# Column sums of the RMS norms on all partitions by one matmul, and the power taken on 512 columns

## The chip, the cores and the metric

The kernel runs on one core of one Trainium2 chip. The metric is the device time of one execution in microseconds (us); of several executions the median is taken. The engines are named as in the profile: PE (TensorE, matrix products), DVE (VectorE), ACT (ScalarE), POOL (GpSimd, which here also issues the stores) and SP (SyncE, which issues the loads). Each engine works through its own instructions in the order in which they were written into its queue; an instruction that waits holds up everything behind it on that engine.

## The reference

A two-layer backbone on 2048 tokens of width 1024. Each layer normalises its rows, modulates them by a conditioning vector, runs a mixer (layer 0 a chunked gMLP, layer 1 multi-scale pooling) and adds the gated result; a last norm ends it. The norm is what the change touches:

```python
def _rmsnorm(x, g):
    xf = x.astype(jnp.float32)
    y = xf * lax.rsqrt(jnp.mean(xf * xf, axis=-1, keepdims=True) + NORM_EPS)
    return (y * g.astype(jnp.float32)).astype(x.dtype)
...
for i in range(DEPTH):            # 2 layers
    h = _rmsnorm(x, norm_g[i]) * (1 + scale[:, None]) + shift[:, None]
    ...
    x = x + gate[:, None] * y
return _rmsnorm(x, final_g)
```

## The kernel before

The stream is held transposed: the 1024 channels are 8 tiles of 128 partitions, tokens run along the free dimension, in blocks of 512. The large products are built from 512x512 quarters in a Strassen-like scheme (seven products for eight), and each float32 product is three matmuls over a high and a low part (`mm3`, L107 to L109). The high and low parts of each weight tile are made on the fly: ACT casts the high part (`whi`, L113) and DVE subtracts it to get the low one (`wlo`, L114). There are nine such pairs of buffers (NPAIR). PE's results go into eight PSUM banks (one tag, bufs=8) and are collected by DVE additions (L700 to L715) and ACT copies.

The program has these stages: the fusion of two pool weights (`fuse`, about 0 to 120 us), and then for each half of the tokens of layer 0 the v products, the u and gate products with the spatial mixing (`b_phase0`), and the output products (`c_pairs`); then the same for layer 1 (`b_phase1`, `c_pairs`, and the last output products in three pieces of 388, 388 and 256 columns, `LAST`). The norms are side work. Their steps are put into a list and taken one by one between the matmul groups. A tile scheduler then lays out each engine's order by priority and by its own costs, so that a step's instructions may be moved among their neighbours.

A norm of n tokens (class `Rms`) first squares the 8 row tiles on ACT and adds them on DVE into one tile `acc` (tag `ra`, one buffer). `root` (L506) then sums over the partitions with one matmul per 128 tokens: the 128x128 slice of `acc` is the stationary operand and one column of ones the moving one, so that the 512 sums land as 128 partitions x 4 columns. On this small tile DVE forms mean plus epsilon (L519), POOL raises it to the power -0.5 (L484, inside `rsqrt`), and four small DVE instructions (L485 to L488) do one Newton step. `diagonals` (L522) writes four 128x128 diagonal matrices on DVE (L528), and `spread` (L531) multiplies ones by them (L536), which puts each token's root on all partitions; ACT copies the bank to `rrow` (L541). The last norm reads the bank directly (`keep`). `rrow` is what `modulate` (L599) and `final_out` (L1171) multiply with.

There are 13 norms: two inside the fusion (at 44 and 97 us), two in each of the two `b_phase0` and of the first `b_phase1` (six), two of 508 columns in the second `b_phase1`, and three in `LAST`. POOL's queue holds, beside these powers, the stores of the stages: `wf_d` (L735), `v_d` (L840), `y_d` (L935, L958, L1130, L1134), `x_d` (L997) and `out` (L1172).

Of the kernel before, what the change touches and what calls it, by code (L numbers as in the profile page):

```python
# [12 lines left out]
F32 = mybir.dt.float32  # L13
F32R = mybir.dt.float32r
AF = mybir.ActivationFunctionType
ALU = mybir.AluOpType

P = 128
D = 1024
# [6 lines left out]
EPS = 1e-6  # L26
# [37 lines left out]
def hybrid_kernel(ctx: ExitStack, tc: tile.TileContext, a: dict):  # L64
    nc = tc.nc
# [3 lines left out]
    sp = ctx.enter_context(tc.tile_pool(name="sp", bufs=2))  # L69
# [24 lines left out]
    def work(tag, width=512):  # L94
        return wk.tile([P, WK[tag][0]], F32, name=tag, tag=tag, bufs=WK[tag][1])[:, 0:width]

    def bank(name="ps"):
        return ps.tile([P, 512], F32, name=name, tag="ps")

    def part(pair, *idx):  # L100
        return tuple(t[idx] for t in pair)
# [3 lines left out]
    def mm3(out, w, x, first, last, onto=False):  # L105

        nc.tensor.matmul(out, w[0], x[0], start=first and not onto, stop=False, skip_group_check=onto)  # L107
        nc.tensor.matmul(out, w[0], x[1], start=False, stop=False, skip_group_check=onto)  # L108
        nc.tensor.matmul(out, w[1], x[0], start=False, stop=last, skip_group_check=onto)  # L109
# [18 lines left out]
    def do_side(n=1000):  # L128
        for _ in range(min(n, len(side))):
            side.popleft()()  # L130
# [282 lines left out]
    ones = cst.tile([P, P], F32, name="ones")  # L413
    nc.gpsimd.memset(ones, 1.0)
    nhalf = cst.tile([P, 8], F32, name="nhalf")
# [66 lines left out]
    def rsqrt(out, v, tmp):  # L482
        pw, cols = v.shape
        power = nc.gpsimd.tensor_tensor(out, v, nhalf[:pw, 0:cols], ALU.pow).ins  # L484
        nc.vector.tensor_mul(tmp, out, out)  # L485
        nc.vector.tensor_mul(tmp, tmp, v)
        nc.vector.tensor_scalar(tmp, tmp, -0.5, 1.5, ALU.mult, ALU.add)
        nc.vector.tensor_mul(out, out, tmp)  # L488
        return power


    class Rms:
        def __init__(self, n, acc, sq):
            self.n, self.acc_tag, self.sq_tag = n, acc, sq

        def square(self, x, first):
            n = self.n
# [3 lines left out]
            else:  # L501
                sq = work(self.sq_tag, n)
                nc.scalar.activation(sq, x, AF.Square)
                nc.vector.tensor_add(self.acc, self.acc, sq)

        def root(self):  # L506
            n = self.n
            nt = (n + P - 1) // P
            pc = bank("pss")
            for t in range(nt):  # L510
                w = min(P, n - t * P)
                nc.tensor.matmul(pc[:w, t:t + 1], self.acc[:, t * P:t * P + w], ones[:, 0:1], start=True, stop=True)
            msq = sp.tile([P, 4], F32, name="msq")
            self.r = sp.tile([P, 4], F32, name="r0")
            tmp = sp.tile([P, 4], F32, name="r1")
            for lo_t, hi_t, w in ((0, n // P, P), (n // P, nt, n % P)):
                if hi_t > lo_t:
                    s = slice(lo_t, hi_t)
                    nc.vector.tensor_scalar(msq[:w, s], pc[:w, s], 1.0 / D, EPS, ALU.mult, ALU.add)  # L519
                    self.pow = rsqrt(self.r[:w, s], msq[:w, s], tmp[:w, s])  # L520

        def diagonals(self):  # L522
            n = self.n
            self.dg = []
            for o in range(0, n, P):
                w = min(P, n - o)
                dg = self.acc[:w, o:o + w]
                nc.vector.tensor_scalar_mul(dg, ident[:w, :w], self.r[:w, o // P:o // P + 1])  # L528
                self.dg.append(dg)

        def spread(self, keep=False):  # L531
            n = self.n
            pr = bank("pr")
            for t, dg in enumerate(self.dg):
                w = min(P, n - t * P)
                nc.tensor.matmul(pr[:, t * P:t * P + w], ones[:w, :], dg, start=True, stop=True)  # L536
            if keep:
                self.out = pr[:, 0:n]
                return
            self.out = sp.tile([P, 512], F32, name="rrow", tag="rrow", bufs=2)[:, 0:n]  # L540
            nc.scalar.copy(self.out, pr[:, 0:n])  # L541
# [6 lines left out]
    def src0(b):  # L548
        return lambda d: a["xT"][d, :, b * TB:(b + 1) * TB]

    def src1(b):
        return lambda d: x1_d[d, :, b * TB:(b + 1) * TB]

    def fetched_rms(src, n, acc, sq, wait=0, kept=None):

        rms = Rms(n, acc, sq)

        def fetch(d):
            x = work(sq if kept is None else "g", n)
            load(x, src(d))  # L560
            if kept is not None:
                kept.append(x)
            return x

        row = ahead(KD, fetch, 1)

        def step(d):
            x = row(d)
            if d == 0 or kept is not None:
                rms.square(x, d == 0)  # L570
            else:
                nc.scalar.activation(x, x, AF.Square)
                nc.vector.tensor_add(rms.acc, rms.acc, x)

        pause = [lambda: None] * wait
        return rms, ([partial(row, 0)] + [partial(step, d) for d in range(KD)] + pause
                     + [rms.root] + pause + [rms.diagonals] + pause + [rms.spread])
# [231 lines left out]
    rms, steps = fetched_rms(src0(1), TB, "ra", "x", 0, others)  # L809
# [160 lines left out]
    def residual(d, x, po, gate, turns=True):  # L970

        g = gate[:, 16 + d:17 + d]
        if d % 2 == 0 or not turns:
            nc.vector.scalar_tensor_tensor(x, po, g, x, ALU.mult, ALU.add)
        else:
            t = work("th", x.shape[1])
            nc.scalar.activation(t, po, AF.Copy, scale=g)
            nc.vector.tensor_add(x, x, t)
# [51 lines left out]
    for b in (2, 3):  # L1030
        rms, steps = fetched_rms(src0(b), TB, "ra", "x", 5)
# [15 lines left out]
    for b in (0, 1):  # L1047
        rms, steps = fetched_rms(src1(b), TB, "ra", "x", 5)
# [127 lines left out]
    for b in (2, 3):  # L1176
        rms, steps = fetched_rms(src1(b), TB, "ra", "x", 5)
# [6 lines left out]
    wide = []  # L1184
# [29 lines left out]
    for j, (t0, n) in enumerate(LAST):  # L1214
        iy, iw = jc2[j]
        tiles = [work(tag, 1048) for tag in ("pc", "pc", "pc", "sw")]
        xt = [tiles[d // 2][:, (d % 2) * n:(d % 2) * n + n] for d in range(KD)]
        rms = Rms(n, "ra", "x")
        last = j == len(LAST) - 1
        for dh in range(2):  # L1220
            for d in range(4 * dh, 4 * dh + 4):
                nc.scalar.dma_start(xt[d], x1_d[d, :, t0:t0 + n])
            po = [bank("po") for _ in range(4)]
            for c in range(0, NC, 2):
                for i in range(4):
                    for cc in (c, c + 1):
                        mm3(po[i][:, 0:n], part(st.get(iw[dh][cc]), every, slice(i * P, (i + 1) * P)), st.get(iy[cc]),
                            cc == 0, cc == NC - 1)
                    if i % 2:
                        do_side(1)  # L1230
            for i in range(4):
                d = 4 * dh + i
                residual(d, xt[d], po[i][:, 0:n], mod[1], not last)
                rms.square(xt[d], d == 0)
        do_side()
        engs = (nc.sync, nc.scalar) if last else (nc.gpsimd, nc.gpsimd)
        pause = [] if last else [lambda: None] * 3
        side.extend(pause + [rms.root] + pause + [rms.diagonals] + pause + [partial(rms.spread, last)]
                    + [partial(final_out, rms, xt[d], d, t0, n, engs[d % 2]) for d in range(KD)])
# [58 lines left out]
```

## Time and profile before

| what | value |
|---|---|
| median of 3 runs | 2400.96 us (2400.38 to 2401.84) |
| the profiled execution: its own time | 2402.3 us |
| its span in the profile | 2400.5 us |
| PE busy | 99% of the span |
| DVE busy | 83% |
| ACT busy | 46% |
| POOL busy | 17% |
| mean granted TensorE clock | 0.994 of full speed |

The profiled execution is 1.3 us above the median, and 1.8 us of its time lie outside the span. A busy share says only how much of the span an engine had an instruction running; matmuls overlap, so PE's rows of about 390 ns for 512 columns follow each other every 230 ns. What an engine waited for stands in the views of waits.

### The profile page before, as it was taken

The numbers are of one execution on the slowest core, as the hardware profiler recorded it, in microseconds if no ns is written. First come the engines' busy times: TensorE is split into PE (matmuls) and PEld (weight loads), VectorE is DVE, ScalarE is ACT, GpSimd is POOL, SyncE is SP. The second block draws the span as 40 slices with busy tenths as digits, with TensorE's granted clock in tenths as the row PEclk, the third lists the DMA queues.
The fourth block names the chain that finished last, engine by engine and source line by source line (L and its number), as shares of the span: only waits on it lengthen the run. The fifth ranks groups of instructions, "written<-read, shape, count | busy, mean of one in ns | idle before, by whom it ended". The sixth has DMA issues, their size and how long they took to land.

```text
span 2400.5 us, 33322 instructions
## 1 busy us (share of the span) xinstructions
PE 2367.3 (99%) x11104; PEld 1994.1 (83%) x11104; DVE 1982.4 (83%) x3323; ACT 1093.0 (46%) x1886; POOL 400.2 (17%) x742
## 2 busy tenths in 40 slices
PE   8999999999999999999999999999999999999998
PEld 7768888888878888888888788888887888888998
DVE  6898788889888668889998869899989688898555
ACT  5744545444555435544346543333356433324433
POOL 2224301010101441113301011112111010100001
PEclk9999999999999999999999999999999999999999
DMA  9647734545777775447857764445487745446664
GB/s 377 248 163 249 254 123 152 169 159 178 244 255 261 245 247 162 151 141 239 271 182 260 250 231 157 150 145 171 144 268 245 234 141 171 144 134 206 208 194 133
DMA packets 204765, 483.41 MB, mean 201 GB/s; under 512 B 27168, under 2 KB 52768, under 8 KB 203568
## 3 DMA queue, kind: packets, MB, share of 16 engines
q1 hardware_dynamic: 152784, 314.00, 41.1%
q0 software_dynamic: 47776, 162.52, 19.1%
q10 hardware_dynamic: 4032, 4.75, 0.7%
q8 instruction: 88, 1.44, 0.2%
q14 instruction: 85, 0.70, 0.1%
HBM read 356.47 MB, written 124.70 MB: 200 GB/s over the span
## 4 chain that ended last, share of the span: by engine, by line
PE 80%; DMA 7%; DVE 6%; issue 4%; POOL 1%; ACT 1%; SPq 1%; DVEq 0%; POOLq 0%; ACTq 0%
PE pu L107 17%; PE pu L109 17%; PE pu L108 17%; PE po L109 7%; PE po L107 7%; PE po L108 7%; PE psp L917 2%; DVE wlo L114 2%; DMA xb<-in_xT 1%; PE pa L107 1%; PE pa L108 1%; PE pa L109 1%; DMA g<-x_d 1%; DMA raw<-to_d 1%; PE pv L107 1%
## 5 line engine op out<-in xcount | busy, mean ns | idle before, releaser
L113 ACT CAST whi<-raw 128x512 fp32r<-128x512 f32 (+1 forms) x960 | 563.6, 617 | 588.2 <-PE pu L108 228.9
L114 DVE TENSOR_TENSOR wlo<-raw,whi 128x512 fp32r<-128x512 f32 (+1 forms) x960 | 632.3, 684 | 126.8 <-ACT whi L113 122.4
L107 PE MATMUL pu<-S,whi 128*128 128x512 f32 x1024 | 400.5, 391 | 0.0
L109 PE MATMUL pu<-S,wlo 128*128 128x512 f32 x1024 | 398.6, 389 | 0.0
L108 PE MATMUL pu<-S,whi 128*128 128x512 f32 x1024 | 398.6, 389 | 0.0
L107 PE MATMUL pu<-A,whi 128*128 128x512 f32 x768 | 300.4, 391 | 0.0
L109 PE MATMUL pu<-A,wlo 128*128 128x512 f32 x768 | 299.0, 389 | 0.0
L108 PE MATMUL pu<-A,whi 128*128 128x512 f32 x768 | 298.8, 389 | 0.0
L109 PE MATMUL po<-whi,wlo 128*128 128x512 f32 (+1 forms) x672 | 263.7, 392 | 6.3 <-DVE wlo L114 6.2
L107 PE MATMUL po<-whi 128*128 128x512 f32 (+1 forms) x672 | 262.4, 391 | 0.0
L108 PE MATMUL po<-wlo,whi 128*128 128x512 f32 (+1 forms) x672 | 262.3, 390 | 0.0
L109 PEld LDWEIGHTS pu<-S,wlo 128*128 128x128 f32 x1024 | 192.2, 188 | 40.3
L107 PEld LDWEIGHTS pu<-S,whi 128*128 128x128 f32 x1024 | 192.3, 188 | 39.2
L108 PEld LDWEIGHTS pu<-S,whi 128*128 128x128 f32 x1024 | 192.3, 188 | 39.2
L109 PEld LDWEIGHTS pu<-A,wlo 128*128 128x128 f32 x768 | 144.1, 188 | 30.3
L108 PEld LDWEIGHTS pu<-A,whi 128*128 128x128 f32 x768 | 144.2, 188 | 29.6
L107 PEld LDWEIGHTS pu<-A,whi 128*128 128x128 f32 x768 | 144.2, 188 | 29.3
L109 PEld LDWEIGHTS po<-whi,wlo 128*128 128x128 f32 x672 | 126.5, 188 | 37.5 <-DVE wlo L114 11.1
L108 PEld LDWEIGHTS po<-wlo,whi 128*128 128x128 f32 x672 | 126.5, 188 | 26.6
L107 PEld LDWEIGHTS po<-whi 128*128 128x128 f32 x672 | 126.6, 188 | 26.3 <-ACT whi L113 0.4
L107 PE MATMUL po<-big,whi 128*128 128x388 f32 (+1 forms) x384 | 123.2, 321 | 0.0
L108 PE MATMUL po<-big,whi 128*128 128x388 f32 (+1 forms) x384 | 122.8, 320 | 0.0
(261 smaller groups left out, 4074.4 us busy)
## 6 DMA issues: line engine op xcount, KB each, us to landing
raw<-in_p_wo SPq DMA_DIRECT2D x120, 256.0 KB, 3.5
raw<-y_d SPq DMA_DIRECT2D x112, 256.0 KB, 3.8
v_d<-g POOLq DMA_DIRECT2D x64, 256.0 KB, 3.8
raw<-in_g_wu SPq DMA_DIRECT2D x32, 512.0 KB, 4.3
raw<-in_g_wg SPq DMA_DIRECT2D x32, 512.0 KB, 4.6
raw<-v_d SPq DMA_DIRECT2D x32, 512.0 KB, 4.6
y_d<-s POOLq DMA_DIRECT2D x64, 256.0 KB, 2.7
x<-in_ada_w SPq DMA_DIRECT2D x64, 256.0 KB, 3.3
```

The costliest lines, as they stand in the source:

```text
L107: nc.tensor.matmul(out, w[0], x[0], start=first and not onto, stop=False, skip_group_check=onto)
L108: nc.tensor.matmul(out, w[0], x[1], start=False, stop=False, skip_group_check=onto)
L109: nc.tensor.matmul(out, w[1], x[0], start=False, stop=last, skip_group_check=onto)
L113: nc.scalar.copy(pair[0], src)
L114: nc.vector.tensor_sub(pair[1], src, pair[0].bitcast(F32))
L917: nc.tensor.matmul(p[:, t * P:(t + 1) * P], vt[h][:, t * 2 * P + j * P:t * 2 * P + (j + 1) * P], bw[:, 0:P], start=True, stop=True)
```

## The change

The class gets a second way, `root_wide`, used by 12 of the 13 norms (the last of `LAST` keeps the old way). One matmul with a 128x128 block of ones as the stationary operand and the whole of `acc` as the moving one puts each token's sum on all 128 partitions at once. DVE scales it out of PSUM (into `acc` again), POOL takes the power on the whole 128x512 tile, straight into `rrow`, and the four Newton instructions run on 128x512. `diagonals` and `spread` do nothing then. The steps stay in the side lists at their places.

```diff
     class Rms:
-        def __init__(self, n, acc, sq):
-            self.n, self.acc_tag, self.sq_tag = n, acc, sq
+        def __init__(self, n, acc, sq, wide=True):
+
+            self.n, self.acc_tag, self.sq_tag, self.wide = n, acc, sq, wide
...
+        def root_wide(self):
+            n = self.n
+            pc = bank("pss")[:, 0:n]
+            nc.tensor.matmul(pc, ones, self.acc, start=True, stop=True)
+            v, t = self.acc, work(self.sq_tag, n)
+            nc.vector.tensor_scalar(v, pc, 1.0 / D, EPS, ALU.mult, ALU.add)
+            out = self.out = sp.tile([P, 512], F32, name="rrow", tag="rrow", bufs=2)[:, 0:n]
+            self.pow = nc.gpsimd.tensor_tensor(out, v, nhalf[:, 0:1].broadcast_to([P, n]), ALU.pow).ins
+            nc.vector.tensor_mul(t, out, out)
+            nc.vector.tensor_mul(t, t, v)
+            nc.vector.tensor_scalar(t, t, -0.5, 1.5, ALU.mult, ALU.add)
+            nc.vector.tensor_mul(out, out, t)
+
         def root(self):
+            if self.wide:
+                return self.root_wide()
...
         def diagonals(self):
+            if self.wide:
+                return
...
         def spread(self, keep=False):
+            if self.wide:
+                return
...
-        rms = Rms(n, "ra", "x")
         last = j == len(LAST) - 1
+        rms = Rms(n, "ra", "x", not last)
```

The two pieces below are the same place of the program, the first norm of the first `b_phase0` (328 us in the trace before), on DVE. `pss` is the bank with the sums, `msq` and `r_` the small tiles of the old way, `raw` and `t_` weight quarters, `wlo` the low parts that PE's products need, `pu` a bank of PE. DVE before:

```order
L700 TENSOR_TENSOR g<-g,pu 128x512
L519 TENSOR_SCALAR msq<-pss 128x4
L194 TENSOR_TENSOR raw<-raw,t_3119 128x512
L485 TENSOR_TENSOR r_3028<-r_3027 128x4
L199 TENSOR_TENSOR raw<-raw 128x512
L486 TENSOR_TENSOR r_3028<-r_3028,msq 128x4
L487 TENSOR_SCALAR r_3028<-r_3028 128x4
L488 TENSOR_TENSOR r_3027<-r_3027,r_3028 128x4
L528 TENSOR_SCALAR ra<-ident,r_3027 128x128 x4
L114 TENSOR_TENSOR wlo<-raw,whi 128x512
```

DVE at the same place now (lines behind L490 of the old file have moved down by up to 20: L720 is the old L700, L725 the old L705, L940 the old L920):

```order
L720 TENSOR_TENSOR g<-g,pu 128x512
L512 TENSOR_SCALAR ra<-pss 128x512
L194 TENSOR_TENSOR raw<-raw,t_3085 128x512
L199 TENSOR_TENSOR raw<-raw 128x512
L515 TENSOR_TENSOR x<-rrow 128x512
L516 TENSOR_TENSOR x<-x,ra 128x512
L114 TENSOR_TENSOR wlo<-raw,whi 128x512
L517 TENSOR_SCALAR x<-x 128x512
L114 TENSOR_TENSOR wlo<-t_3085,whi 128x512
L518 TENSOR_TENSOR rrow<-rrow,x 128x512
L114 TENSOR_TENSOR wlo<-raw,whi 128x512
L725 TENSOR_TENSOR g<-g,pu 128x512
```

The diagonals are gone; L515, the first reader of the power's result, stands two instructions behind L512, with the low parts and the bank collection of the unit behind it.

On POOL, at the same norm, before (`rs` is the variance root of the v stage, `y_d` the stores of `b_phase0`):

```order
L484 TENSOR_TENSOR rs<-ve,nhalf 128x8
L958 DMA y_d<-s 128x512 x2
L935 DMA y_d<-g 128x512
L958 DMA y_d<-s 128x512
L935 DMA y_d<-s 128x512
L935 DMA y_d<-g 128x512 x2
L484 TENSOR_TENSOR r_3027<-msq,nhalf 128x4
L958 DMA y_d<-s 128x512 x2
```

And now:

```order
L484 TENSOR_TENSOR rs<-ve,nhalf 128x8
L978 DMA y_d<-s 128x512 x2
L955 DMA y_d<-g 128x512
L978 DMA y_d<-s 128x512
L955 DMA y_d<-s 128x512
L955 DMA y_d<-g 128x512 x2
L514 TENSOR_TENSOR rrow<-ra,nhalf 128x512
L978 DMA y_d<-s 128x512 x2
```

The power stands at the same place of POOL's queue, on 512 columns where it had 4, with the next chunk's stores behind it.

## Rows read from the trace of the kernel before

**Rows 1.** The page's busy time: engine, us, share of the span, instructions.
```profile
PE 2367.3 (99%) x11104; PEld 1994.1 (83%) x11104; DVE 1982.4 (83%) x3323; ACT 1093.0 (46%) x1886; POOL 400.2 (17%) x742
```
**Rows 2.** The waits of PE, longest first: total us, times, longest.
```profile
PE po L109 <- DVE wlo L114: 6.2, 4, 2.6
PE pss L512 <- DVE ra L504: 5.1, 2, 3.6
```
**Rows 3.** Timeline of PE: the spread, a 512-column float32 matmul, the sums, two mm3.
```profile
53.34 1.05 PE L536 MATMUL pr<-ra,ones 128*128 128x128 f32 x8
...
130.34 1.02 PE L791 MATMUL pw<-ra,ones 128*128 128x512 f32 x2
...
327.19 0.95 PE L512 MATMUL pss<-ones,ra 128*128 128x1 f32 x8
...
328.54 0.40 PE L109 MATMUL pu<-A,wlo 128*128 128x512 f32 x1
...
329.24 0.39 PE L109 MATMUL pu<-A,wlo 128*128 128x512 f32 x1
```
**Rows 4.** Groups of DVE instructions: busy us, mean ns, idle before.
```profile
L599 DVE TENSOR_TENSOR g<-g,rrow 128x512 f32<-128x512 f32 x40 | 26.3, 686 | 28.3 <-DMA g<-x_d 14.7 <-DMA g<-in_xT 12.9 <-ACT rrow L541 0.7
...
L462 DVE TENSOR_SCALAR ra<-x,cond 128x512 f32<-128x512 f32 x8 | 4.1, 512 | 2.4 <-DMA tp_d<-ra 2.4
```
**Rows 5.** Timeline of POOL: the power on 4, 8, 4, 8 and 2 columns.
```profile
44.19 1.04 POOL L484 TENSOR_TENSOR r<-msq,nhalf 128x4 f32<-128x4 f32 x1 [8.85 <-DVE msq L519]
...
285.10 2.03 POOL L484 TENSOR_TENSOR rs<-ve,nhalf 128x8 f32<-128x8 f32 x1 [1.30 <-DVE ve L882]
...
328.42 1.40 POOL L484 TENSOR_TENSOR r<-msq,nhalf 128x4 f32<-128x4 f32 x1 [0.60 <-DVE msq L519]
...
937.17 2.08 POOL L484 TENSOR_TENSOR rs<-ve,nhalf 128x8 f32<-128x8 f32 x1 [2.86 <-DVE ve L882]
...
2390.93 0.72 POOL L484 TENSOR_TENSOR r<-msq,nhalf 128x2 f32<-128x2 f32 x1 [17.25 <-DVE msq L519]
```
**Rows 6.** Other POOL work on SBUF tiles, groups: busy us, mean ns, idle before.
```profile
L1119 POOL COPY keep_g<-g 128x8 f32<-128x8 f32 x16 | 6.3, 396 | 48.4 <-ACT g L1162 48.4
L1153 POOL COPY keep<-pc 128x16 f32<-128x16 f32 x16 | 8.5, 532 | 69.5 <-DVE pc L708 59.2 <-DVE pc L711 10.3
L414 POOL MEMSET ones<- 128x128 f32 x1 | 0.2, 224 | 0.0
```
**Rows 7.** Timeline of DVE, beside an 8-column power and around the norm at 328 us.
```profile
284.93 0.68 DVE L573 TENSOR_TENSOR ra<-ra,x 128x512 f32<-128x512 f32 x1
...
328.18 0.16 DVE L519 TENSOR_SCALAR msq<-pss 128x4 f32<-128x4 f32 x1
328.25 0.68 DVE L194 TENSOR_TENSOR raw<-raw,t 128x512 f32<-128x512 f32 x1
329.86 0.16 DVE L485 TENSOR_TENSOR r<-r 128x4 f32<-128x4 f32 x1 [0.92 <-POOL r L484]
...
331.13 0.87 DVE L528 TENSOR_SCALAR ra<-ident,r 128x128 f32<-128x128 f32 x4
```
**Rows 8.** The waits of DVE: total us, times, longest.
```profile
DVE wlo L114 <- ACT whi L113: 132.4, 96, 6.0
...
DVE r L485 <- POOL r L484: 12.7, 17, 1.2
```
**Rows 9.** The waits of ACT.
```profile
ACT whi L113 <- PE pu L108: 228.9, 148, 4.6
```
**Rows 10.** The waits of POOL.
```profile
POOL y_d L958 <- DVE s L956: 346.8, 31, 27.7
```
**Rows 11.** Stretches: length, busy us PE, PEld, DVE, ACT, POOL; PE clock, DMA, GB/s.
```profile
36.00:42.00 6.00, 2.44 (x12) 1.68 (x10) 4.29 (x5) 2.50 (x4) 0.00 (x0) 0.89 1.03 405
42.00:44.00 2.00, 2.00 (x9) 2.00 (x10) 0.13 (x1) 0.00 (x0) 0.00 (x0) 0.50 1.05 429
44.00:47.00 3.00, 3.00 (x8) 2.32 (x8) 1.64 (x9) 1.17 (x2) 2.06 (x3) 0.50 1.01 401
```

## The prediction

> **What bounds the kernel now.** I read the busy shares first, then who waited for whom, then the groups and the timeline around the norms. PE is busy 99% of the span, DVE 83%, POOL 17% [rows 1]. PE hardly waits: its longest entry is 6.2 us in four pieces, for a low part from DVE [rows 2]. So the kernel ends when PE has issued its matmuls, and anything else costs only where it starves PE. Two engines can do that. DVE makes the low parts and empties PE's banks. POOL issues the stores that free the buffers. A reader should look at one number above all: how long DVE waits at L485, the first reader of the power. It is 12.7 us over 17 waits, at most 1.2 us each [rows 8], which is the power on a few columns less the one or two instructions that the scheduler put in between [rows 7].
>
> **PE and ACT.** The old way takes on PE 0.95 us for the sums and 1.05 us for the spread of a norm [rows 3]. The new single matmul, ones as the stationary operand and 512 float32 columns moving, has its twin in the trace: the bias step's `pw` takes 1.02 us [rows 3]. So PE saves 0.95 + 1.05 - 1.02 = 1.0 us a norm, 12 us over 12 norms, and these lie on the path, since PE is the bound. ACT loses one copy a norm; ACT is busy 46% [rows 1], so I count nothing.
>
> **DVE's work.** Gone are five small instructions of about 0.16 us and the diagonals with 0.87 us [rows 7], some 1.7 us. New are three products of 128x512 at 0.69 us and two scalings at 0.51 us [rows 4], 3.1 us; the scaling out of PSUM has no row of its own and stands at the value of the one from SBUF. That is 1.4 us more a norm, 17 us in all, on an engine with 17% idle. By itself it is hidden; it counts once, in the catch-up below.
>
> **The power.** POOL now raises 512 columns where it raised 4. The trace has the same instruction on 2, 4 and 8 columns [rows 5]. 2 columns take 0.72 us and 4 take 1.04 us with DVE quiet beside it, 0.16 us a column. Where a two-operand DVE instruction runs across the start [rows 7], 4 columns take 1.40 us and 8 take 2.03 and 2.08 us, again (2.055 - 1.40) / 4 = 0.164 us a column. Both pairs agree and the increment doesn't shrink from 2 to 8. The line is 0.40 us + 0.162 us a column. At 512 columns it gives 83.3 us, at 508 82.7 us, at 388 63.3 us. No row shows it beyond 8 columns, so both ends: from above the 8-column row taken as a plain proportion, 2.055 / 8 = 0.257 us a column, 131 us at 512; from below POOL's copies, 0.396 us for 8 and 0.532 us for 16 columns, 0.017 us a column and some 9 us at 512, and below them the memset of 128 columns in 0.224 us, about 0.9 us at 512 [rows 6]. I take 0.162, since it comes from the same instruction on the same operands. Eight norms have 512 columns, two 508, two 388: 8 x 83.3 + 2 x 82.7 + 2 x 63.3 = 958 us of POOL time.
>
> The Trainium skill speaks against such a price: "GPSIMD Engine Reference", section 3.1, puts a two-operand elementwise instruction of this engine at about 2.6 cycles of 1.2 GHz for each element along the free dimension. By that, an estimate from that page, 512 columns are 1.1 us and the sum would come out at the 2389 us of the first rival below. The trace does not agree for this operation: 0.16 us a column is some seventy times that figure; the page's measurement is of an add.
>
> **Where the power falls.** It stalls two queues at once. On DVE, L515 waits for it, and the order shows only two instructions between the scaling and L515 at the first norm of `b_phase0`; at the other norms it is none to three. Behind L515 stand the splits that PE's next products need and the additions that empty its banks. DVE can't pass the wait, so it is shut for nearly the whole power. On POOL the next stores stand behind the power. There the stores of a chunk come after waits of up to 27.7 us [rows 10], so 83 us would make them late by some 55 us; but DVE, which makes their data, stands still for the same 83 us, so I count this stall once. It is what is late next if DVE's wait is taken away.
>
> How long does PE go on while DVE stands? One product of four mm3 takes 4 x 0.69 = 2.8 us [rows 3]. At least 6.0 us are covered: DVE has waited that long for a cast [rows 8] in a kernel whose PE waits for low parts are 6.2 us in all [rows 2]. At most the nine pairs hold some eight products, 22 us, and so do the eight banks. Casts do wait for PE to free a pair, 228.9 us in 148 waits [rows 9], so pairs are often full; but the root at 328 us stands amid a unit's subtractions, when the splits that follow are not made yet, and the spatial matmuls take four banks at once. I take 10 us, nearer to the low end. After the power, DVE has the four Newton instructions, 0.69 + 0.69 + 0.51 + 0.69 = 2.6 us, mixed with the first split: 3 us of catch-up. And PE restarts slowly: after its idle time between 36 and 42 us (2.44 us busy of 6) the granted clock was 0.50, the 1.2 GHz level, over the next 5 us [rows 11], which costs half of them, 2.5 us. A norm thus costs PE its power - 10 + 3 + 2.5 = power - 4.5 us.
>
> **The sum.** Against the profiled execution of 2402.3 us (span 2400.5 us and 1.8 us around it): + 958 (powers) - 12 x 4.5 = 54 (cover, catch-up, clock) - 12 (matmuls) = + 892, so 3294 us. That execution is 1.3 us above the median of the runs, so I forecast 3293 us. With the cover at 22 us it is 12 x 12 = 144 us less, 3149 us; at 6 us it is 48 us more, 3341 us.
>
> **Rivals.**
> 1. The power streams on wide tiles (not slower). If its 0.162 us a column is the price of a short instruction only and the wide one runs near the copies' 0.017 us, it takes 9 us or less, DVE's wait stays within the cover of 10 us, and what is left is the 12 us of PE: 2401 - 12 = 2389 us. The deciding point is about 10 us a power, 0.02 us a column. For it: nothing wider than 8 columns was ever measured, and the copies and the memset are that cheap [rows 6]. Against it: an equal price for the third and fourth and for the fifth to eighth column [rows 5]. Chance 0.07; with the extra DVE work and a wait a little over the cover it would end within 0.2% of before, chance 0.03 more.
> 2. The price falls with length, say to half, 0.081 us: 958 becomes 482 us, and the sum 2817 us. Nothing in the trace shows a fall from 2 to 8 columns. Chance 0.07 for anything between 0.03 and 0.13 us a column.
> 3. The power is dearer, by the plain proportion 0.257 us a column or by sharing ports with DVE: the rows with a DVE instruction beside them are 0.36 us longer [rows 5]. DVE stands still here, which speaks against it. 8 x 131 + 2 x 130 + 2 x 100 = 1508 us instead of 958: 3843 us. Chance 0.05.
>
> **How the numbers follow.** The forecast (power on the line of 0.162, cover between 6 and 22 us) has 0.78; its own range is 3150 to 3345 us, and a price of 0.155 to 0.17 us widens that by some 45 us on either side. Rivals 1 and 2 lie far below and are left out, with 0.17 together; of rival 3 the nearer half comes in. The range is 3060 to 3480 us, which leaves out about 0.2. A time within 0.2% of before is what a measurement of this kernel can't tell from no change. Faster by over 0.2%: 0.07 (rival 1). Within: 0.03. Slower: 0.78 + 0.07 + 0.05 = 0.90.
>
> **What would show it.** The power's rows at L514 show the price: about 83 us on 512 and 63 us on 388 columns would be right, and POOL's busy time near 400 + 950 us. DVE's wait at L515 should be within a few us of that, 12 times, some 930 us in the view of waits. PE should wait about 12 times for 55 to 75 us on low parts, banks or casts, and show the 0.50 clock behind each. DVE's busy time should rise by only about 17 us. The forecast is wrong if L514 takes under 60 us on 512 columns, or if it is that long and PE's waits at a norm are yet shorter than 50 us, which would mean that more work stands ahead of L515 than I count. If PE's waits are longer than the power, the stores behind it on POOL add a stall of their own.

## The result, and the profile after

The changed kernel takes 3278.1 us (median of 4 runs, 3272.9 to 3280.8) against 2400.7 us before: ratio 1.3657, 95% interval 1.3641 to 1.3673, slower by 877 us. The forecast was 3293 us, the range 3060 to 3480 us.

The page's busy time answers to [rows 1]. The span is 3271.1 us.

```profile
PE 2388.7 (73%) x10936; PEld 1997.7 (61%) x10936; DVE 1997.6 (61%) x3255; ACT 1071.0 (33%) x1874; POOL 1330.1 (41%) x738
```

PE, DVE and ACT do almost the work of before. POOL does 930 us more, and PE is idle for 3271.1 - 2388.7 = 882 us where it was idle for 33 us. The groups of POOL (busy us, mean ns, idle before) show the power, which answers to [rows 5]:

```profile
L514 POOL TENSOR_TENSOR rrow<-ra,nhalf 128x512 f32<-128x512 f32 x8 | 657.7, 82209 | 41.0 <-DVE ra L512 41.0
L514 POOL TENSOR_TENSOR rrow<-ra,nhalf 128x508 f32<-128x508 f32 x2 | 163.1, 81553 | 22.1 <-DVE ra L512 22.1
L514 POOL TENSOR_TENSOR rrow<-ra,nhalf 128x388 f32<-128x388 f32 x2 | 124.8, 62423 | 115.3 <-DVE ra L512 115.3
```

82.2 us on 512 columns and 62.4 us on 388 are (82.2 - 62.4) / 124 = 0.160 us a column; the twelve add up to 945.6 us. The first row of DVE's waits (total, times, longest) answers to the second of [rows 8]: one wait per power, nearly as long as the power.

```profile
DVE x L515 <- POOL rrow L514: 929.1, 12, 81.8
```

PE's waits answer to [rows 2]. Each norm leaves one long wait, on whichever product of DVE comes first in PE's order, a low part (L114) or an emptied bank (L725, L732, L940), or on ACT, which itself stood behind DVE:

```profile
PE pf L109 <- DVE wlo L114: 154.7, 6, 78.5
PE pu L107 <- DVE g L725: 152.5, 4, 76.9
PE po L109 <- DVE wlo L114: 113.8, 9, 54.2
PE pu L107 <- DVE g L732: 74.3, 1, 74.3
PE pu L107 <- DVE pc L725: 74.2, 1, 74.2
PE pu L109 <- DVE wlo L114: 74.0, 2, 73.1
PE pu L107 <- DVE s L940: 72.3, 1, 72.3
PE pu L107 <- ACT ra L501: 67.3, 1, 67.3
PE pu L107 <- ACT whi L113: 64.8, 1, 64.8
```

These nine rows are 848 us. In the row of L501 it is the next norm's first square: it writes the one buffer of `ra`, which the power and L516 still read, and started 0.1 us after L516 ended, with the rest of ACT's queue behind it. So the power stalled ACT too at this norm:

```profile
1355.12 0.63 ACT L501 ACTIVATE ra<-x 128x512 f32<-128x512 f32 x1 [82.63 <-issue]
```

The timeline of the first norm of `b_phase0`, three lines picked from POOL, DVE and PE (start, length, instruction, idle time before it), shows one in full; it is the place of [rows 7]:

```profile
487.81 82.32 POOL L514 TENSOR_TENSOR rrow<-ra,nhalf 128x512 f32<-128x512 f32 x1 [1.20 <-DVE ra L512]
...
570.16 0.69 DVE L515 TENSOR_TENSOR x<-rrow 128x512 f32<-128x512 f32 x1 [80.40 <-POOL rrow L514]
...
574.98 0.80 PE L107 MATMUL pu<-S,whi 128*128 128x512 f32 x1 [73.49 <-DVE g L725]
```

PE ran on until 574.98 - 73.49 = 501.5 us, 13.7 us into the power, and started again 4.9 us after the power's end. Read in the same way, the twelve norms differ widely: PE ran on for 4.8 to 21.7 us (mean 12.7) and started again 1.4 to 5.3 us after the power's end (mean 3.2). The shortest and the longest run-on are these (POOL's power, then PE's restart):

```profile
173.07 81.95 POOL L514 TENSOR_TENSOR rrow<-ra,nhalf 128x512 f32<-128x512 f32 x1
...
256.40 0.80 PE L109 MATMUL pf<-whi,wlo 128*128 128x512 f32 x1 [78.50 <-DVE wlo L114]
...
2553.27 81.78 POOL L514 TENSOR_TENSOR rrow<-ra,nhalf 128x508 f32<-128x508 f32 x1
...
2639.85 0.76 PE L107 MATMUL pu<-A,whi 128*128 128x512 f32 x1 [64.85 <-ACT whi L113]
```

The twelve long waits add up to 832 us. The stretches around the wait that ends at 574.98 us (columns as in [rows 11]) show PE's clock at the 1.2 GHz level behind it; over the first 3 us behind each of the other eleven the granted clock is 0.50 as well:

```profile
501.00:574.00 73.00, 0.49 (x3) 0.07 (x1) 3.81 (x7) 0.57 (x2) 69.13 (x1) 0.54 0.00 0
574.00:578.00 4.00, 3.02 (x7) 2.46 (x8) 4.00 (x7) 0.00 (x0) 0.00 (x0) 0.50 0.00 0
578.00:580.00 2.00, 2.00 (x9) 1.60 (x9) 2.00 (x6) 0.00 (x0) 0.00 (x0) 0.94 0.15 45
```

### The profile page after: what moved, and what is told of

Same layout as the page of the kernel before. It is cut to its first block, busy times and chain, and to the rows that moved or that the text cites. A ratio compares the mean times of both kernels' runs of the same rounds, so it can differ in the third digit from the quotient of the medians.

```text
span 3271.1 us, 32942 instructions
## 1 busy us (share of the span) xinstructions
PE 2388.7 (73%) x10936; PEld 1997.7 (61%) x10936; DVE 1997.6 (61%) x3255; ACT 1071.0 (33%) x1874; POOL 1330.1 (41%) x738
## 5 line engine op out<-in xcount | busy, mean ns | idle before, releaser
L514 POOL TENSOR_TENSOR rrow<-ra,nhalf 128x512 f32<-128x512 f32 (+2 forms) x12 | 945.6, 78802 | 178.4 <-DVE ra L512 178.4
L113 ACT CAST whi<-raw 128x512 fp32r<-128x512 f32 (+1 forms) x960 | 554.6, 615 | 678.5 <-DVE raw L194 308.3
L114 DVE TENSOR_TENSOR wlo<-raw,whi 128x512 fp32r<-128x512 f32 (+1 forms) x960 | 635.5, 688 | 108.5 <-ACT whi L113 103.2
L107 PE MATMUL pu<-S,whi 128*128 128x512 f32 x1024 | 407.0, 397 | 305.4 <-DVE g L725 152.5
L515 DVE TENSOR_TENSOR x<-rrow 128x512 f32<-128x512 f32 (+2 forms) x12 | 8.0, 670 | 929.1 <-POOL rrow L514 929.1
L107 PE MATMUL pu<-A,whi 128*128 128x512 f32 x768 | 305.4, 398 | 204.4 <-DVE s L940 72.3
L108 PE MATMUL pu<-S,whi 128*128 128x512 f32 x1024 | 402.8, 393 | 0.0
L108 PE MATMUL pu<-A,whi 128*128 128x512 f32 x768 | 302.3, 394 | 0.0
L107 PEld LDWEIGHTS pu<-A,whi 128*128 128x128 f32 x768 | 146.4, 191 | 236.9 <-DVE s L940 72.7
L109 PEld LDWEIGHTS pu<-A,wlo 128*128 128x128 f32 x768 | 146.3, 191 | 104.6 <-DVE wlo L114 73.8
L109 PE MATMUL po<-big,wlo 128*128 128x388 f32 (+1 forms) x384 | 125.4, 327 | 104.1 <-DVE wlo L114 104.0
L978 POOL DMA_DIRECT2D y_d<-s x48 | 26.2, 547 | 371.2 <-DVE s L976 346.4
L1182 ACT ACTIVATE g<-g 128x512 f32<-128x512 f32 x64 | 40.5, 632 | 390.7 <-DVE sw L1118 89.5
L109 PE MATMUL pf<-whi,wlo 128*128 128x512 f32 x128 | 53.5, 423 | 154.7 <-DVE wlo L114 154.7
```

What stands on the lines that cost most here:

```text
L113: nc.scalar.copy(pair[0], src)
L114: nc.vector.tensor_sub(pair[1], src, pair[0].bitcast(F32))
L514: self.pow = nc.gpsimd.tensor_tensor(out, v, nhalf[:, 0:1].broadcast_to([P, n]), ALU.pow).ins
L515: nc.vector.tensor_mul(t, out, out)
L978: nc.gpsimd.dma_start(y_d[bb, c, (0, 1, None, 3)[j]], ss[j])
L1182: nc.scalar.activation(gt[j], gt[j], AF.Silu)
```

## The experiments

The theory: DVE, which takes its queue in order, stands at L515 for the length of the power, and PE starves for that length less a constant. The rivals: POOL's queue, with the stores behind the power, sets the stall; or the wide tiles cost by themselves. The edits are cut to the lines that matter.

**Power on 8, 64 and 256 columns.** The other columns get a constant; matmul, scaling and Newton step stay wide. (k is 8, 64, 256.)

```diff
+            nc.gpsimd.memset(out[:, k:n], 0.01)
-            self.pow = nc.gpsimd.tensor_tensor(out, v, nhalf[:, 0:1].broadcast_to([P, n]), ALU.pow).ins
+            self.pow = nc.gpsimd.tensor_tensor(out[:, 0:k], v[:, 0:k], nhalf[:, 0:1].broadcast_to([P, k]), ALU.pow).ins
```

> Leaves out the power of all but the first 8 columns of each wide norm (the others are set to a constant). Everything else is the changed kernel: wide matmul, wide scaling, wide Newton step. Theory (the stall is DVE's wait for the power): about 2389 us, that is before less 12 us of PE, between 2385 and 2398; DVE's wait for the power at most 3 us a norm. Rival (the wide tiles themselves cost: 1.4 us more of DVE a norm, the bank, the buffer held): 2410 us or more.

> Leaves out the power beyond 64 columns. The power should take 0.4 + 64 x 0.159 = 10.6 us. Theory with a cover of 10 us before PE starves: hardly any stall, 2389 to 2420 us. If the cover is only 6 us: 12 x (10.6 - 6 + 3) = 91 us more, about 2480 us. This run measures the cover.

> Leaves out the power beyond 256 columns. The power should take 0.4 + 256 x 0.159 = 41.1 us. Theory: each norm costs the power less 8 us (cover less catch-up, as the changed kernel shows) plus 2.8 us of slow clock, 12 x 36 = 431 us over 2389, about 2820 us, DVE's wait some 12 x 40 us. Rival (the stores queued on POOL behind the power set the stall, and 27 us of lateness is free there): 12 x 14 = 170 us, about 2560 us.

Measured: 2392.4 us with 8 columns (ratio to before 0.9967, interval 0.9954 to 0.9980), 2467.6 us with 64 (1.0277, 1.0260 to 1.0293), 2836.8 us with 256 (1.1824, 1.1807 to 1.1841). The power's group in the three, in this order:

```profile
L515 POOL TENSOR_TENSOR rrow<-ra,nhalf 128x8 f32<-128x8 f32 x12 | 24.3, 2021 | 193.7 <-DVE ra L512 193.7
```
```profile
L515 POOL TENSOR_TENSOR rrow<-ra,nhalf 128x64 f32<-128x64 f32 x12 | 130.7, 10890 | 183.4 <-DVE ra L512 183.4
```
```profile
L515 POOL TENSOR_TENSOR rrow<-ra,nhalf 128x256 f32<-128x256 f32 x12 | 497.7, 41472 | 182.3 <-DVE ra L512 182.3
```

From 8 to 64 columns a column costs 0.158 us, from 64 to 256 it costs 0.159 us, and from 256 to 512 again 0.159 us: a straight line. The first run shows that the wide tiles cost nothing: all of the change but the power is worth a small gain. The page of that run has

```profile
PE 2355.2 (98%) x10936; PEld 1978.8 (83%) x10936; DVE 1996.2 (83%) x3255; ACT 1083.9 (45%) x1874; POOL 414.8 (17%) x750
```

PE's busy time is 12.1 us under that of [rows 1]. Above the time of this run, 64 columns cost 75 us, 256 cost 444 us, and the change as it is 886 us. Per norm these are 6.3, 37.0 and 73.8 us for powers of 10.9, 41.5 and 78.8 us (the mean of the twelve): the power less 4.5 to 5 us, all along the line. The second run was expected at 2389 to 2420 us for a cover of 10 us, and at about 2480 us for one of 6 us; it came near the second. What missed was to let the cover hide a power of 10 us whole. The page of that run has a span of 2469.8 us and

```profile
PE 2375.0 (96%) x10936; PEld 1985.3 (80%) x10936; DVE 1991.5 (81%) x3255; ACT 1068.4 (43%) x1874; POOL 522.0 (21%) x750
```

so PE idles 94.8 us, 59 us more than with 8 columns (36.0 us), and is busy 20 us longer with the same matmuls. The catch-up after the power counts even where the cover is longer than the power, as at the first norm of `b_phase0`:

```profile
346.61 10.92 POOL L515 TENSOR_TENSOR rrow<-ra,nhalf 128x64 f32<-128x64 f32 x1 [1.20 <-DVE ra L512]
...
362.86 0.50 PE L107 MATMUL pu<-S,whi 128*128 128x512 f32 x1 [2.56 <-DVE g L726]
```

PE ran on until 360.3 us, 13.7 us into the power as in the changed kernel and 2.8 us past its end, and still stood for 2.6 us, since DVE had not yet emptied the bank. The 256-column run speaks against the stores as the cause: it took 2837 us, where the theory had about 2820 us and the stores about 2560 us.

**The stores moved off POOL.** In the changed kernel and, as the control, in the kernel before, the y stores of the mixing stages go to SP's queue:

```diff
-            nc.gpsimd.dma_start(y_d[bb, k, pn - 1], out)
+            nc.sync.dma_start(y_d[bb, k, pn - 1], out)
...
-                nc.gpsimd.dma_start(y1_d[k, pn - 1], out)
+                nc.sync.dma_start(y1_d[k, pn - 1], out)
```

> The changed kernel with the y stores of the mixing stages issued by SP instead of POOL, so that no such store stands behind a power. Theory (DVE's wait alone sets the stall): 3278 us plus what the move itself costs, which the kernel before with the same move (e8_before_stores) shows against 2401 us; the difference between the two stays near 877 us. Rival (stores behind the power set the stall of the ten norms outside the last stage): the difference falls to 400 us or less.

> The kernel before with the y stores of the mixing stages issued by SP instead of POOL: the control of e5_stores and e7_defer_stores. All theories: 2400 us if SP has time for them, up to some 100 us more where a store waiting for its data holds up the loads behind it.

Measured: 3276.8 us (1.3655, 1.3615 to 1.3695) and, for the control, 2390.2 us (0.9957, 0.9937 to 0.9977). The difference between the two is 887 us, against 877 us without the move. DVE's wait is the same:

```profile
DVE x L515 <- POOL rrow L514: 929.8, 12, 81.8
```

Here, while DVE stands, a free store queue is worth nothing. That rules out the rival in which the stores set the stall of the changed kernel.

**DVE's wait moved away.** The Newton step is issued as a step of its own, 35 side steps behind the power, and held in program order there; once with the stores on POOL and once with them on SP. The edit also takes out the pause of five side steps between the squares and the column sums, so the sums come earlier.

```diff
+        def newton(self):
+            n, v, out, t = self.n, self.acc, self.out, work(self.sq_tag, self.n)
+            tc.keep_in_program_order(nc.vector.tensor_mul(t, out, out))
...
         def spread(self, keep=False):
             if self.wide:
-                return
+                return self.newton()
...
-        pause = [lambda: None] * wait
-        return rms, ([partial(row, 0)] + [partial(step, d) for d in range(KD)] + pause
-                     + [rms.root] + pause + [rms.diagonals] + pause + [rms.spread])
+        pause = [lambda: None] * (35 if wait else 0)
+        return rms, ([partial(row, 0)] + [partial(step, d) for d in range(KD)]
+                     + [rms.root] + pause + [rms.spread])
```

> The whole computation; the Newton step, and with it DVE's first read of the power, is put 35 side steps later and kept there, which leaves DVE 55 to 173 instructions before it at the eight norms of the mixing stages (none more at the two of the fusion and the two of the last stage). DVE's wait should fall to about 2 x 80 + 46 + 16 + 41 + 34 + 2 x 61 us, some 420 us, with none at the four norms of layer 1's mixing. Theory with stores that cost nothing: about 2392 + 390 = 2780 us. Theory with the stores as what is late next, as the prediction has it (55 us at the norms of layer 0's mixing, up to 40 us at those of layer 1's): about 3040 us. Rival (DVE's wait doesn't matter, POOL's queue does): 3250 us or more.

> As e6_defer, and the y stores issued by SP: neither DVE nor a store waits behind the power at the norms of layer 1's mixing. Theory: about 2780 us, plus the cost of the move itself (e8_before_stores). If e6_defer is near 3040 us and this one near 2780 us, the stores were what came next.

Measured: 3074.9 us (1.2814, 1.2776 to 1.2851) and 2981.8 us (1.2425, 1.2389 to 1.2461). Both compute the whole reference. The first came near the 3040 us of the theory with late stores. DVE's waits in it:

```profile
DVE x L518 <- POOL rrow L514: 272.4, 4, 77.4
DVE s L943 <- issue: 177.5, 4, 52.7
...
DVE pc L723 <- ACT pc L721: 92.0, 3, 43.3
DVE g L1152 <- POOL keep_g L1142: 73.5, 1, 73.5
DVE pc L1126 <- POOL keep L1176: 72.2, 1, 72.2
```

The wait for the power is left at the four norms where it could not be moved. At the four norms of layer 0's mixing DVE now waits 36 to 53 us to write `s` (L943), the tile that the y stores free; at the two norms of 508 columns L723 waits 43 us each, behind an ACT copy into a `pc` tile that such a store had to free. That the time came near the theory's 3040 us is in part luck: the stores were to cost up to 4 x 55 + 4 x 40 = 380 us, but they show 177.5 + 86 us in DVE's waits, and the other 146 us (L1152, L1126) are no stores, as the next run shows. With the stores on SP it reads:

```profile
DVE x L518 <- POOL rrow L514: 377.1, 8, 77.4
...
DVE g L1152 <- POOL pc L1165: 73.5, 1, 73.5
DVE pc L1126 <- POOL keep L1176: 72.1, 1, 72.1
DVE sw L1111 <- POOL pc L1168: 53.8, 2, 28.0
```

L943 is gone from the list and L723 has one wait of 8.0 us left, at another place, so the long ones were the stores; what is left at the norms of layer 0's mixing is the power again, up to 42 us. But this run missed its 2780 us by 202 us. I had counted only stores as POOL's other work. The rows show what I left out: POOL's tiny copies and memsets of the pooling edges (`keep`, `keep_g`, the edge of `pc`), which stand behind the power as well and which DVE needs at once. At the two 512-column norms of layer 1's mixing DVE stands 72 to 74 us for them, and at the two of 508 columns 26 to 28 us. Two of PE's waits in this run belong to the 202 us as well:

```profile
PE pss L510 <- DVE ra L596: 43.4, 3, 14.8
PE pm L470 <- DVE ra L464: 37.1, 2, 22.4
```

The first is for the last addition before the column sums, which the edit put closer together; the second is for the sums of the conditioning vector. How the 202 us divide among these and the copies stays open: no run has this edit with a short power.

**The root without POOL.** Square root on ACT and reciprocal on DVE in place of the power; and the same with the stores on SP.

```diff
-            self.pow = nc.gpsimd.tensor_tensor(out, v, nhalf[:, 0:1].broadcast_to([P, n]), ALU.pow).ins
+            nc.scalar.activation(t, v, AF.Sqrt)
+            self.pow = nc.vector.reciprocal(out, t).ins
```

> The whole computation, with the power on 512 columns replaced by a square root on ACT and a reciprocal on DVE. Theory: nothing waits for POOL any more, and the 12 us of PE come out: 2389 us, between 2385 and 2400, if the reciprocal costs DVE no more than some 3 us a norm and the two changes of ACT's function table no more than some 3 us a norm, both under the cover. Rival (the wide way costs by itself): 2410 us or more.

> The whole computation, e4_actsqrt (square root on ACT, reciprocal on DVE) with the y stores issued by SP as in e8_before_stores. If the two gains add, 2401 - 7 - 9 = 2385 us, between 2380 and 2391, under both kernels. If the store move gained only because of something that e4 has gained already, 2390 to 2394 us.

Measured: 2393.6 us (0.9968, 0.9955 to 0.9981) and 2384.8 us (0.9939, 0.9926 to 0.9953). Both compute the whole reference. The second is 15 us under the kernel before and the fastest here; the gains of the two parts add (7 us and 9 us). The reciprocal is dear, 3.35 us of DVE on 512 columns, but in the first of the two its row has almost no idle time before it, and PE is idle for 38.7 us of the span of 2394.6 us, about as with the 8-column power:

```profile
L515 DVE RECIPROCAL rrow<-x 128x512 f32<-128x512 f32 x8 | 26.8, 3348 | 2.0 <-ACT x L514 2.0
```
```profile
PE 2355.9 (98%) x10936; PEld 1979.5 (83%) x10936; DVE 2028.7 (85%) x3267; ACT 1110.8 (46%) x1903; POOL 383.3 (16%) x726
```

## Why the prediction was right

The mechanism, its place and its size held; the sum was 21 us above the change of the profiled spans (892 against 3271.1 - 2400.5 = 871 us). Term by term:

- The power: 958 us forecast, 945.6 us measured. The straight line from 2 to 8 columns, 0.162 us each, held up to 512 at 0.159. Rivals 1 and 2, the streaming power and the one that gets cheaper with length, are shown wrong by the line over 8, 64, 256 and 512 columns; rival 3 by the same rows. The figure of the Trainium skill ("GPSIMD Engine Reference", section 3.1), an estimated 1.1 us for 512 columns from its add, does not carry over to this operation: 82.2 us were measured.
- DVE's wait: some 930 us forecast, 929.1 us in 12 waits measured. With the power cut to 8 columns the stall is gone, and with POOL's stores taken from behind it nothing changes. With the wait moved away at eight norms the time fell by 203 us, and by 296 us without the stores; it fell no further because four norms kept their wait and POOL's other work then made DVE wait at the rest, so no run takes this wait away alone.
- Cover less catch-up: 10 - 3 = 7 us a norm forecast. PE's idle time grew by 882 - 33 = 849 us, so it is (945.6 - 849) / 12 = 8.0 us. That the two lie so close is in part luck. PE ran on for 12.7 us on the mean, not 10, and between 4.8 and 21.7 us, so the 6.0 us that the prediction took as a least cover is not one. The catch-up was about right, 3.2 us on the mean. The long waits alone would give (945.6 - 832) / 12 = 9.5 us; smaller waits of PE, the other 17 us of the 849 us, bring it down to 8.0; the prediction has no term for them.
- The slow clock: 2.5 us a norm forecast. PE's busy time is 2388.7 us against 2355.2 us with the same matmuls and the 8-column power, 33.5 us or 2.8 us a norm.
- The matmuls: 12 us forecast, 12.1 us less PE busy time in the 8-column run. Its time fell by 8 us, not 12: in the profiled spans 9.3 us arrive (2400.5 - 2391.2), as PE idles 2.8 us more than before (36.0 against 33.2 us).
- DVE's extra work: 17 us forecast, 1997.6 - 1982.4 = 15 us measured, hidden as expected.

What failed is a number inside rival 1: the point from which the power decides, put at 10 us. It is cover less catch-up, on the mean some 6 us by the 64-column run, where powers of 10.9 us left PE idle for 59 / 12 = 4.9 us each; and it is no single point, since in the changed kernel the long wait is 3.5 to 16.9 us shorter than its power, depending on the norm. PE's waits were also wider spread than the 55 to 75 us named, 49.6 to 78.5 us. And "what is late next" was too narrow: the stores alone were named, at 55 us a norm. The run with the Newton step moved showed 36 to 53 us for them, and beside them POOL's small copies with 73 us, more than the stores.

## What to carry to other kernels

Before an instruction is made wider, read its rows at several widths in the trace: if each column costs the same at 2, 4 and 8, reckon with that price at 512, as it came out here, and measure one wider case. A long instruction on a lightly loaded engine is paid where another engine's queue first reads its result; look in the order at what stands between, and then at everything else in the slow engine's own queue, copies as well as stores. Replicating a sum over the partitions to save two small steps also replicates the elementwise work behind it, here from 4 columns to 512.

## What the runs showed of the hardware

POOL's power is linear in the columns, 0.159 us each from 8 to 512. DVE's reciprocal on 128x512 takes 3.35 us where a product takes 0.69 us. Moving the y stores from POOL's to SP's queue made the kernel before 9 us faster (0.9957, 0.9937 to 0.9977), with 6 us less PE busy time and 6 us less PE idle time; I had expected no gain, and its cause stays open.
